# A hybrid short-convolution and RG-LRU layer in fp32r: one output product of the second half made from seven smaller ones, and the order of the opening and of the sweeps

## The chip, the cores and the metric

The kernel runs on one core of one Trainium2 chip. The metric is device microseconds (us) of one execution; the time of a kernel is the median of its runs. The engines are named as the profile names them: PE (TensorE), DVE (VectorE), ACT (ScalarE), POOL (GpSimd), SP (SyncE, which issues transfers here).

## The reference

One layer of a diffusion trunk on 2048 latent tokens of width 1024, with 256 context tokens whose scan states start the latent scans.

```python
shift, scale, gate = split(silu(c) @ w_ada + b_ada, 3)
h  = rmsnorm(x, norm_g) * (1 + scale) + shift            # hc: the same of ctx with c_ctx
v, g_b, g_c, z_a, u, z_b, m_a, m_b = split(h @ w_in)     # eight products 1024 x 1024
xc = grid_conv(u, conv4_w, 2) + conv4_b                  # rows of 64 tokens
r, i = sigmoid(block_diag(xc, wr) + br), sigmoid(block_diag(xc, wi) + bi)   # per direction
a = exp(-8 * r * softplus(-lambda)); y_lru = scan_fwd + scan_bwd of sqrt(1-a*a) * i * xc
y_a = g_b * grid_conv(g_c * v, conv3_w, 1) * silu(z_a)
y_b = y_lru * silu(z_b)
merged = sigmoid(m_a) * (y_a @ w_out_a) + sigmoid(m_b) * (y_b @ w_out_b)
x = rmsnorm(x + gate * (merged @ w_o), final_g)
```

## The kernel before

The tokens lie in four blocks of 512. A tile is 128 channels by 512 tokens. Blocks 0 and 1 are the first half, blocks 2 and 3 the second. Every product is made in fp32r with weights and data split into a high and a low part: high by high, low by high and high by low are added up, so a product with a full inner dimension of 1024 takes 24 matmuls for one output tile (`passes`, line 455).

Where two blocks and both halves of the channels come together, a 2 x 2 scheme with seven products (`Pair`, line 524) takes the place of the eight plain ones. Each of the seven takes 12 matmuls. It needs seven forms of the data: B11, B21 and B22, which are tiles as they are, and T1 to T4, which are differences (T1 = x12-x11, T3 = x22-x12, T2 = x22-T1, T4 = x21-T2). It also needs four weight differences, made by four POOL instructions in `prep_d` (line 540). Loops over such products are `sgemm` (line 1127); loops over plain products are `gemm` (line 1114).

The program goes in this order. (1) The opening: the adaLN rows are made by matvecs with the loaded rows `wc` of w_ada (line 841); block 0 is modulated two channel tiles at a time as its scale and shift arrive (`modulated`); then the plain products aL, aG, aV, aMA, aB, aZA of the first channel tile are made, first with block 0, then with block 1. (2) `sweep(0, c)` for the eight channel tiles c, each with seven products for each of the L, G, B and Z weights, the LRU gates (`bdp`, `Lru.gates`) and the forward scans. (3) The first half's product with w_out_a (`merged_a(0)`), in which the forms of the second half are built. (4) `sweep(1, c)`, with the backward scans of the first half (`back0`) and `gate_step` recorded after each sweep. (5) The second half's product with w_out_a (`merged_a(1)`, names `oa1..`, plain), in which the forms of y_b are built (`build_y`, DVE). (6) `merged_b(1)` with w_out_b (names `ob1..`, seven products), `wo1`, `merged_b(0)`, and the last product with w_o and the output.

Nothing of this runs in the order in which it is recorded. Each call adds an `Op` with an engine and an estimated duration to a `Plan`, and `place` and `once` (lines 125 and 141) list-schedule them: PE keeps the order of recording, the other engines take the ready Op of the lowest priority number, which is the latest time by which the Ops after it need it. Buffers come from slot pools: 17 T slots (fp32 tiles), 64 F slots (fp32r tiles, the data's parts), W, D, R and S for weights, six accumulators. A load is issued no earlier than 18 us ahead of its priority (`AHEAD`).

A form from DRAM is loaded into a T slot; then ACT writes the high part and DVE the low part into two F slots (`put`, line 423).

Of the kernel before, what the change touches and what calls it, by code (L numbers as in the profile page):

```python
# [25 lines left out]

PARAMS = (("g", K), ("bada", 3 * K), ("w3", 3 * K), ("w4", 4 * K), ("b4", K), ("br", 2 * K),
# [45 lines left out]
class Op:  # L73
    def __init__(self, eng, dur, emit, table=None, lat=0.15):
        self.eng, self.dur, self.emit, self.table, self.lat = eng, dur, emit, table, lat
        self.deps, self.succ, self.allocs, self.uses = set(), [], [], []
        self.prio = self.nom = self.start = self.end = 0.0


class Plan:  # L80
# [60 lines left out]
    def once(self):  # L141
# [6 lines left out]
        indeg = {op: len(op.deps) for op in ops}  # L148
# [27 lines left out]
        while len(order) < len(ops):  # L176
            best = None
            now = pe[pe_at].nom if pe_at < len(pe) else 1e9
            for e, c in cand.items():
                pick = None  # L180
                for op in c:
# [3 lines left out]
                    if op.allocs:  # L185
                        if e == "SP" and op.prio > now + AHEAD:
                            continue
# [37 lines left out]
            for b in op.uses:  # L225
                b.left -= 1
                b.end = max(b.end, op.end + op.lat)
                if not b.left and b.pool:
                    insort(slots[b.pool], (b.end, b.slot))
            for s in op.succ:  # L230
# [16 lines left out]
def trunk(ctx: ExitStack, tc: tile.TileContext, par, sel2, xT, ctxT, wada, wgate, crow, win, woa, wob, wo, lru, out):  # L247
# [110 lines left out]
    yb_dram = dram("yb_dram", 2, K, 2, P, T)  # L358
    mg_dram = dram("mg_dram", 2, K, 2, P, T)
# [59 lines left out]
    def split2(hi, lo, x, n=T):  # L419
        A(hi, x, AF.Copy, n=n)  # L420
        TT(lo, x, hi, SU, n)
# [10 lines left out]

    def fetch(name, src, kb=512, after=()):
# [4 lines left out]
    def plain(name, src, after=()):  # L438
        r = fetch("r" + name, src, after=after)
# [4 lines left out]
    def spread(name, src, after=()):  # L444

        r = fetch("r" + name, src, after=after)
# [370 lines left out]
    last = []  # L817

    def wload(m):
        for k in range(K):  # L820
            w = wc[m, k] = tb(f"wc{m}{k}")
            last[:] = [DMA(w.v, wada[m, :, k, :], 256)]

    def xload(name, src):
        r = []
        for k in range(K):
            x = tf(f"{name}{k}")
            last[:] = [DMA(x.v, src[:, k, :], 256, after=[sel_op])]
            r.append(x)
        return r  # L830
# [45 lines left out]
    acc0 = [ps(n) for n in ("aL", "aG", "aV")]  # L876
# [13 lines left out]

    rv = matvec(0)
    wload(1)
    turn(0, rv)
    rv = matvec(1)
    rs0 = s0.rs()
    modulated(0)
    ws0[0] = wL = plain("L00", sL, after=last)
    wload(2)
    turn(1, rv)
    modulated(1)  # L900
    rv = matvec(2)
    ws0[1] = wG = plain("G00", sG, after=last)
    turn(2, rv)
    wload(3)
    ws0[2] = wV = plain("V00", sV, after=last)
    group(0, 0)
    modulated(2)
    group(0, 1)
    rv = matvec(3)
    group(0, 2)  # L910
    turn(3, rv)
    modulated(3)
    wMA = spread("MA00", sMA, after=last)
    wB = spread("B00", sB, after=last)
# [4 lines left out]
    for i in (1, 2):  # L919
        for m in range(H - 1):  # L920
            group(i, m)
    for i in range(3):
# [4 lines left out]
    wZA = spread("ZA00", sZA, after=last)  # L927
    a = unit("aMA0", wMA, bt0)
    merge_gate("sma_dram", 0, 0, 0, a.v)
    rs1 = s1.rs()  # L930
# [14 lines left out]
    for j in range(H):  # L945
        h = tb(f"hcx{j}")
        DMA(h.v, ctxT[:, 2 * j:2 * j + 2, :].rearrange("p k n -> p (k n)"), 256, after=last)
# [3 lines left out]
    a = unit("aB0", wB, bt0)  # L951
    cv.gb(0, a.v)
# [9 lines left out]
    lr.weights(after=last)  # L962
# [31 lines left out]
    def rest(form, kinds, biased=True):  # L994

        for n, i in kinds:
            for j in range(H):
                x = tb(n + "x")
                DMA(x.v, dbuf("fm_dram", i, j), 256)
                form[n].append(put(f"{n}_{j}", x.v, shf(H + j) if i == 2 and biased else None))  # L1000


    def sweep(half, c, state, form):

        plain_start = half == 0 and c == 0
# [10 lines left out]
        else:  # L1016
# [7 lines left out]
            lr.conv(0, l0.v)  # L1024
            pl.p6(form)
            if half == 0:
                lr.ctx_gates(0)
            pl.p5(form)
            if half == 0:
                lr.ctx_gates(1)  # L1030
                lr.ctx_scan()
            ma1 = pl.p7(form)
# [403 lines left out]
```

## Time and profile before

| | before |
|---|---|
| median of 3 runs | 1954.68 us (1952.62 to 1955.51) |
| profiled execution | 1953.45 us |
| its span in the trace | 1951.7 us (1.75 us lie around it) |
| mean granted clock of PE | 0.994 |
| busy: PE, DVE, ACT, POOL | 97%, 81%, 58%, 26% |

The span is what the profiler records from the first to the last instruction. Busy shares are shares of the span. The profile's line numbers are those of the kernel before; in the kernel after, the helpers have moved (the ACT helper from line 264 to 274, tensor-tensor from 270 to 280, matmul from 312 to 322).

### The profile page before, as it was taken

What the parts mean: (1) busy time and instruction counts of PE and PEld (TensorE: products, weight loads), DVE (VectorE), ACT (ScalarE), POOL (GpSimd) and SP (SyncE); (2) the same over time, 40 slices, a digit from 0 to 9 for tenths busy, and PEclk for the clock granted to TensorE, in tenths of its full rate; (3) what the DMA queues carried; (4) which work ended last, traced back from release to release, by engine and by line L of the source; (5) the groups of instructions that cost most, each with busy time, mean ns of one, the idle gap of its engine ahead of it and who ended that gap; (6) DMA issues with size and microseconds to landing.
All of it is one profiled execution on the core that took longest, in us unless ns stands there. A gap on an engine that the chain in (4) does not pass through costs nothing.

```text
span 1951.7 us, 24306 instructions
## 1 busy us (share of the span) xinstructions
PE 1902.7 (97%) x8546; PEld 1562.0 (80%) x8546; DVE 1578.9 (81%) x2044; ACT 1136.3 (58%) x1604; POOL 503.1 (26%) x311
## 2 busy tenths in 40 slices
PE   6989999999999999999999999999999999999997
PEld 3777888888888888888888888888888888788787
DVE  6897878778686878858998989989898778779854
ACT  5587676767677777347565575655747333435332
POOL 1313223322535221023324333233241022012100
PEclk8999999999999999999999999999999999999999
DMA  9252323232433325951433424234243985777933
GB/s 328 75 184 95 124 81 125 79 131 91 161 119 121 124 81 195 325 189 57 157 109 112 146 75 157 92 129 143 69 167 101 334 316 187 271 244 248 328 119 117
DMA packets 145419, 307.89 MB, mean 158 GB/s; under 512 B 16272, under 2 KB 20496, under 8 KB 145296
## 3 DMA queue, kind: packets, MB, share of 16 engines
q1 hardware_dynamic: 145296, 306.34, 45.5%
q8 instruction: 67, 1.10, 0.2%
q14 instruction: 56, 0.46, 0.1%
HBM read 218.19 MB, written 88.08 MB: 157 GB/s over the span
## 4 chain that ended last, share of the span: by engine, by line
PE 68%; DVE 14%; ACT 8%; DMA 6%; issue 3%; SPq 0%; ACTq 0%; DVEq 0%
PE oa L312 9%; PE wo L312 4%; PE ao L312 4%; PE bdp L312 3%; ACT L264 3%; DVE xc L277 2%; DMA pk<-pk_dram 2%; DVE i L296 2%; PE ac L312 1%; DMA wc<-wada 1%; DVE x L277 1%; DMA mg_dram<-sb 1%; DVE y L270 1%; DVE wg L277 1%; DVE i L270 1%
## 5 line engine op out<-in xcount | busy, mean ns | idle before, releaser
L264 ACT ACT_TABLE_LOAD x152 | 195.0, 1283 | 8.1 <-DMA pr<-par 2.7
L296 DVE TENSOR_TENSOR_SCAN i<-a,st,i 128x512 f32<-128x512 f32 x48 | 75.2, 1579 | 0.0
L270 DVE TENSOR_TENSOR i<-i,r 128x512 f32<-128x512 f32 x64 | 66.7, 1042 | 0.1
L277 DVE SCALAR_TENSOR_TENSOR r<-a,r 128x512 f32<-128x512 f32 x64 | 49.2, 789 | 18.1 <-ACT r L264 18.1
L264 ACT ACTIVATE xh<-xc 128x512 fp32r<-128x512 f32 x32 | 20.2, 632 | 61.7 <-DVE xc L277 61.7
L270 DVE TENSOR_TENSOR i<-i,xc 128x512 f32<-128x512 f32 x64 | 50.4, 806 | 0.4 <-ACT i L264 0.4
L264 ACT ACTIVATE a<-r,ns 128x512 f32<-128x512 f32 x64 | 45.9, 720 | 0.8 <-DVE i L270 0.3
L264 ACT ACTIVATE r<-bdp,pr 128x512 f32<-128x512 f32 x64 | 44.0, 687 | 2.1 <-PE bdp L312 0.6
L264 ACT ACTIVATE i<-bdp,pr 128x512 f32<-128x512 f32 x64 | 44.0, 687 | 0.6 <-PE bdp L312 0.6
L264 ACT ACTIVATE r<-r,hs 128x512 f32<-128x512 f32 x64 | 43.1, 712 | 0.0
L277 DVE SCALAR_TENSOR_TENSOR zz<-ao,gates,xr 128x256 f32<-128x256 f32 (+1 forms) x24 | 13.6, 572 | 34.5 <-PE ao L312 32.6
L264 ACT ACTIVATE sq<-zz 128x256 f32<-128x256 f32 (+1 forms) x21 | 10.3, 488 | 49.4 <-DVE zz L277 49.2
L264 ACT ACTIVATE r<-r 128x512 f32<-128x512 f32 x64 | 37.7, 624 | 0.4
L270 DVE TENSOR_TENSOR xl<-xc,xh 128x512 fp32r<-128x512 f32 x32 | 33.4, 1045 | 4.5 <-ACT xh L264 4.5
L270 DVE TENSOR_TENSOR sa<-oa,sa 128x512 f32<-128x512 f32 x32 | 21.7, 686 | 13.3 <-DMA sa<-sma_dram 7.2
L277 DVE SCALAR_TENSOR_TENSOR ri<-acc,ri 128x256 f32<-128x256 f32 x16 | 6.5, 413 | 30.3 <-ACT ri L264 30.3
L270 DVE TENSOR_TENSOR yx<-yx,yx 128x512 f32<-128x512 f32 x32 | 25.3, 790 | 5.0 <-DMA fm_dram<-yx 2.4
L270 DVE TENSOR_TENSOR y<-y,sg 128x512 f32<-128x512 f32 x32 | 29.0, 907 | 0.0
L841 PE MATMUL row<-wc,sc 128*32 128x512 f32 x64 | 15.8, 698 | 9.5 <-DMA wc<-wada 4.9
L270 POOL TENSOR_TENSOR ob00s<-ob00r 128x512 f32<-128x512 f32 x1 | 1.3, 1292 | 91.5 <-DMA fm_dram<-yx 91.5
L296 DVE TENSOR_TENSOR_SCAN pk<-pk,st,pk 128x512 f32<-128x512 f32 x16 | 20.5, 1279 | 5.2 <-DMA pk<-pk_dram 5.2
L270 POOL TENSOR_TENSOR ob10s<-ob10r 128x512 f32<-128x512 f32 x1 | 1.3, 1289 | 89.6 <-DMA ob10r<-wob 89.6
(15371 smaller groups left out, 7391.3 us busy)
## 6 DMA issues: line engine op xcount, KB each, us to landing
pk<-pk_dram SPq DMA_DIRECT2D x48, 256.0 KB, 5.7
wc<-wada SPq DMA_DIRECT2D x32, 256.0 KB, 5.4
ya_dram<-y SPq DMA_DIRECT2D x32, 256.0 KB, 3.4
pk_dram<-i SPq DMA_DIRECT2D x32, 256.0 KB, 2.8
roa<-woa SPq DMA_DIRECT2D x16, 512.0 KB, 4.3
ya<-ya_dram SPq DMA_DIRECT2D x32, 256.0 KB, 5.1
sa<-sma_dram SPq DMA_DIRECT2D x32, 256.0 KB, 5.0
pa_dram<-sa SPq DMA_DIRECT2D x32, 256.0 KB, 5.0
```

The source lines that it names most:

```text
L264: act.activation(o.ap(), i.ap(), func, **kw)
L270: return plan.add(Op(eng, d, lambda: e.tensor_tensor(o.ap(), a.ap(), b.ap(), op=op)), [o], [a, b])
L277: dve.scalar_tensor_tensor(o.ap(), a.ap(), s.ap() if isinstance(s, V) else s, b.ap(), op0=op0, op1=op1, **kw)
L296: dve.tensor_tensor_scan(o.ap(), a.ap(), u.ap(), init.ap() if isinstance(init, V) else init, op0=M, op1=AD)
L312: pe.matmul(o.ap(), w.ap(), x.ap(), start=a, stop=z, skip_group_check=True)
L841: pe.matmul(row.fixed[32 * j:32 * j + 32, :], w.ap(), x.ap(), start=a, stop=z, skip_group_check=True, tile_position=(0, 32 * j))
```

## The change

It has five parts.

1. The second half's product with w_out_a becomes an `sgemm` of seven products (`merged_a1`). The forms of y_a come from `combine("ya", j)`: four loads, four POOL subtractions and four stores to `yat_dram`, recorded inside the sweeps 5, 6 and 7 for j = 0 to 2; for j = 3 they are made on DVE from tiles still in SBUF. The forms of y_b for `merged_b(1)` come in the same way from `combine("yb", j)`, inside the sweeps 6 and 7 and inside the product, and no longer from `build_y` on DVE. Forms are loaded when they are first asked for, two kinds ahead (`LEAD`), and the low part of j = 1 is made on POOL (`POOLED`).
2. `put_from` loads a form into the F slot of its own low part and not into a T slot.
3. `sweep` takes a list of steps, and `back0`, `gate_step` and `combine` are recorded between its products.
4. In the opening all loads are chained in one order (`queue`): block 0, the first w_ada rows, then weights and rows in turn, and block 1 behind the last rows. The products aMA and aB take part, in groups of two channel tiles, as the modulation arrives. The sums of squares of block 1 move from POOL to DVE.
5. In `sweep(0, 0)` the last gates and forward scan (`late`) are recorded behind the next sweep's first tail product.

```diff
+            if op.heir:
+                op.prio = min(p, op.heir.prio)
...
+    def put_from(name, src, bias=None, eng="DVE"):
+
+        lo, hi = fb(name + "l"), fb(name + "h")
+        raw = lo.m(lambda t: t.bitcast(F32))
+        DMA(raw, src, 256)
+        if bias is None:
+            split2(hi.v, lo.v, raw, eng=eng)
...
+    def queue(op):
+
+        if line:
+            line[-1].heir, op.heir_of = op, line[-1]
+        op.dur *= 0.84
+        line.append(op)
+        return op
...
-    acc0 = [ps(n) for n in ("aL", "aG", "aV")]
+    rL, rG = raw0("L00", sL), raw0("G00", sG)
+    acc0 = [ps(n) for n in ("aL", "aG", "aV", "aMA0", "aB0")]
...
+    rMA = raw0("MA00", sMA)
+    wload(3)
     rv = matvec(2)
...
+    rB = raw0("B00", sB)
     rv = matvec(3)
+    group(3, 0)
     turn(3, rv)
+    group(3, 1)
+    for i in range(4):
+        group(i, 2)
+    ws0[4] = wB = spread("B00", sB, rB)
     modulated(3)
+    for m in range(H - 1):
+        group(4, m)
     x1 = xload("x1_", xT[1])
-    s1 = Stats("x1", eng="POOL")
+    s1 = Stats("x1")
...
+            def late(first=state["tail"][0]):
+                first()
+                lr.gates(1, 1)
+                lr.decay(1)
+                lr.forward(1)
+            state["tail"][0] = late
...
+        for i, (o, a, b) in enumerate(((x11, x12, x11), (x12, x22, x12), (x22, x22, x11), (x21, x21, x22))):
+            TT(o, a, b, SU, eng="DVE" if late else "POOL")
+            if not late:
+                DMA(dbuf(f"{key}t_dram", (0, 2, 1, 3)[i], j), o, 256)
...
     for c in range(K):
-        sweep(1, c, state, form1)
-        if c + 1 < K:
-            gate_step(c)
-            back0(2 * c)
-            back0(2 * c + 1)
+        side = []
+        if c:
+            side = [lambda: back0(2 * c - 2), lambda: gate_step(c - 1), lambda: back0(2 * c - 1)]
+        if c > H:
+            side.insert(1, lambda: combine("ya", c - H - 1))
+        if c > H + 1:
+            side.insert(3, lambda: combine("yb", c - H - 2))
+        sweep(1, c, state, form1, side)
+    y7 = combine("ya", H - 1, [state["cv"].y[t] for t in range(2)])
...
-        if n in (2, 5, 8, 11):
-            build_y(1, n // 3, forms_y[1])
-
-    merged_a(1, ya, between_a)
-    rest(forms_y[1], (("T3", 1), ("T4", 0), ("B22", 2)), False)
-    mg = merged_b(1, forms_y[1], lambda n: None)
+    merged_a1(Forms("ya", y7), between_a)
+    mg = merged_b(1, Forms("yb"), lambda n: None)
```

The order on the engines moves most at three places. The first is ACT in the opening, where `B_0h` and `B_1h` are the high parts of the third pair of block 0's channel tiles, `sq` the squares, and `rows_431` and `rows_494` the copy of the fourth adaLN row. Before, it stands so:

```order
L264 ACTIVATE B_0h<-x_4_188,ab 128x512
L264 ACTIVATE B_1h<-x_5_192,ab 128x512
L264 ACTIVATE V00h<-rV_351 128x1024
L264 ACTIVATE rows_431<-row_389 128x512
L264 ACTIVATE sq<-x_3_366 128x512
L264 ACTIVATE MA000h<-rMA_364 128x512
```

After, it stands so (`ZA000h` is a weight's high part):

```order
L274 ACTIVATE sq<-x_4_347 128x512
L274 ACTIVATE sq<-x_5_351 128x512
L274 ACTIVATE sq<-x_6_354 128x512
L274 ACTIVATE B_0h<-x_4_127,ab 128x512
L274 ACTIVATE B_1h<-x_5_129,ab 128x512
L274 ACTIVATE sq<-x_7_363 128x512
L274 ACTIVATE rows_494<-row_458 128x512
L274 ACTIVATE ZA000h<-rZA_369 128x512
```

The copy of the fourth row stood ahead of block 1's squares 3 to 7; now it stands behind all eight of them.

The second place is POOL in the last sweep and at the start of the second half's w_out_a product. Before, the four differences of the last Z weights are followed by those of the first w_out_b weights:

```order
L270 TENSOR_TENSOR Z17r_12085<-Z17s_12185,Z17r_12085 128x512
L270 TENSOR_TENSOR Z17r_12085<-Z17r_12085 128x512
L270 TENSOR_TENSOR ob10s_13091<-ob10r_13038 128x512
L270 TENSOR_TENSOR ob10r_13038<-ob10r_13044,ob10r_13038 128x512
```

After (`cx` are the tiles of `combine`, `yaB` and `yaT` the parts of y_a's forms, `oa10r` the raw w_out_a weights):

```order
L280 TENSOR_TENSOR Z17r_12121<-Z17s_12233,Z17r_12121 128x512
L280 TENSOR_TENSOR Z17r_12121<-Z17r_12121 128x512
L280 TENSOR_TENSOR yaB_1l<-yaB_1l,yaB_1h 128x512 x2
L280 TENSOR_TENSOR oa10s_12461<-oa10r_12412 128x512
L280 TENSOR_TENSOR oa10r_12412<-oa10r_12320,oa10r_12412 128x512
L280 TENSOR_TENSOR yaT_1l<-yaT_1l,yaT_1h 128x512
L280 TENSOR_TENSOR oa10r_12320<-oa10s_12461,oa10r_12320 128x512
L280 TENSOR_TENSOR yaT_1l<-yaT_1l,yaT_1h 128x512
L280 TENSOR_TENSOR oa10r_12320<-oa10r_12320 128x512
L280 TENSOR_TENSOR yaT_1l<-yaT_1l,yaT_1h 128x512 x2
L280 TENSOR_TENSOR cx_12571<-cx_12575,cx_12571 128x512
```

Between the last Z weights and the first w_out_b weights POOL now makes low parts of the forms, the differences of four pairs of w_out_a weights and subtractions of y_b.

The third place is DVE at the start of that product. Before (`ya_0k` are the plain tiles of y_a, `Z17a`, `Z17u` and `y` the last steps of the last sweep):

```order
L270 TENSOR_TENSOR ya_05l<-ya_05_12434,ya_05h 128x512
L270 TENSOR_TENSOR ya_06l<-ya_06_12453,ya_06h 128x512
L270 TENSOR_TENSOR Z17a<-Z17a,zs_12423 128x512
L270 TENSOR_TENSOR y_12217<-y_12217,sg_12340 128x512
L270 TENSOR_TENSOR Z17a<-Z17a,i_170_12087 128x512
L270 TENSOR_TENSOR Z17u_12374<-Z17z,Z17u_12374 128x512
```

After:

```order
L280 TENSOR_TENSOR y_12263<-y_12263,sg_12472 128x512
L280 TENSOR_TENSOR cx_12470<-cx_12503,cx_12470 128x512
L280 TENSOR_TENSOR yaB_0l<-yaB_0l,yaB_0h 128x512
L280 TENSOR_TENSOR yaB_2l<-yaB_2l,yaB_2h 128x512
L280 TENSOR_TENSOR yaB_3l<-yaB_3l,yaB_3h 128x512
L280 TENSOR_TENSOR cx_12503<-y_12263,cx_12503 128x512
L280 TENSOR_TENSOR oa10Bl<-oa10r_12320,oa10Bh 128x1024
L280 TENSOR_TENSOR y_12263<-y_12263,cx_12470 128x512
L280 TENSOR_TENSOR yaT_0l<-yaT_0l,yaT_0h 128x512
L280 TENSOR_TENSOR yaT_2l<-yaT_2l,yaT_2h 128x512
```

The chain of differences of j = 3 (`cx`, then `y`) now lies on DVE between the last sweep and the product, with the low parts of the forms among it.

## Rows read from the trace of the kernel before

**Rows 1.** The page's busy time, share of the span and instructions of each engine.

```profile
PE 1902.7 (97%) x8546; PEld 1562.0 (80%) x8546; DVE 1578.9 (81%) x2044; ACT 1136.3 (58%) x1604; POOL 503.1 (26%) x311
```

**Rows 2.** Stretches: opening, end of sweeps, second w_out_a product; last: clock, DMA share, GB/s.

```profile
0.00:200.00 200.00, 173.74 (x740) 128.90 (x741) 152.86 (x254) 137.26 (x210) 47.37 (x37) 0.96 0.49 168
900.00:1508.00 608.00, 606.05 (x2667) 499.95 (x2667) 554.35 (x664) 369.99 (x500) 200.59 (x116) 1.00 0.35 118
1508.00:1599.00 91.00, 91.00 (x404) 75.32 (x403) 67.44 (x97) 31.31 (x46) 7.50 (x6) 1.00 0.90 326
```

**Rows 3.** The chain that ended last, PE: start, time, of what.

```profile
1510.98 87.04 PE oa L312 x384
1646.98 2.73 PE ob12y L312 x12
```

**Rows 4.** Stretches of the first 40 us, columns as in rows 2.

```profile
0.00:20.00 20.00, 9.84 (x35) 2.83 (x36) 9.83 (x46) 8.73 (x14) 0.20 (x4) 0.97 0.92 314
20.00:40.00 20.00, 16.54 (x62) 7.78 (x65) 11.98 (x23) 11.30 (x15) 2.07 (x2) 0.69 1.04 392
```

**Rows 5.** Timeline of ACT and PE, opening: start, mean of one, instruction, [wait <-releaser].

```profile
44.31 0.58 ACT L264 ACTIVATE rows<-row 128x512 f32<-128x512 f32 x1
46.34 2.18 ACT L264 ACTIVATE sq<-x 128x512 f32<-128x512 f32 x4
...
76.55 0.58 PE L312 MATMUL aL<-B_0h,L00h 128*128 128x512 f32 x1
79.05 0.50 PE L312 MATMUL aL<-B_1l,L00h 128*128 128x512 f32 x1 [1.01 <-DVE B_1l L277]
84.06 0.50 PE L312 MATMUL aL<-B_3l,L00h 128*128 128x512 f32 x1 [0.63 <-DVE B_3l L277]
141.57 0.78 PE L312 MATMUL bdp<-xh,bw00h 128*128 128x512 f32 x1 [4.97 <-ACT r L264]
```

**Rows 6.** Stretches of PE alone: length, busy, granted clock, DMA share, GB/s.

```profile
34.00:36.00 2.00, 1.28 (x4) 0.50 1.06 398
140.00:142.00 2.00, 0.43 (x1) 0.91 0.00 0
142.00:144.00 2.00, 2.00 (x6) 0.50 0.28 102
144.00:146.00 2.00, 2.00 (x9) 0.74 0.95 294
```

**Rows 7.** Timeline of DVE and POOL near the end of the last sweep, columns as in rows 5.

```profile
1470.45 0.48 DVE L283 TENSOR_SCALAR y<-G17a,pr 128x512 f32<-128x512 f32 x1
1475.49 1.28 POOL L270 TENSOR_TENSOR Z17s<-Z17r 128x512 f32<-128x512 f32 x1 [13.35 <-DMA Z17r<-win]
1475.78 2.08 DVE L270 TENSOR_TENSOR Z17Al<-Z17r,Z17Ah 128x1024 fp32r<-128x1024 f32 x1
1477.78 1.77 DVE L270 TENSOR_TENSOR G17u<-G17u,G17u 128x512 f32<-128x512 f32 x1
1479.48 1.77 DVE L270 TENSOR_TENSOR i<-i,r 128x512 f32<-128x512 f32 x1
1481.18 1.52 DVE L283 TENSOR_SCALAR y<-G17u,pr 128x512 f32<-128x512 f32 x1
1492.06 0.69 DVE L270 TENSOR_TENSOR i<-i,r 128x512 f32<-128x512 f32 x1
1495.18 1.23 DVE L270 TENSOR_TENSOR Z17Cl<-Z17r,Z17Ch 128x1024 fp32r<-128x1024 f32 x1
```

**Rows 8.** Stretches of the sweeps 5, 6 and 7 and of the product, columns as in rows 2.

```profile
1256.00:1338.00 82.00, 81.57 (x360) 67.25 (x359) 74.50 (x89) 49.47 (x67) 27.70 (x17) 1.00 0.34 119
1338.00:1420.00 82.00, 82.00 (x364) 67.91 (x363) 74.62 (x91) 49.70 (x68) 27.13 (x17) 1.00 0.34 119
1420.00:1508.00 88.00, 87.00 (x383) 71.44 (x382) 78.97 (x101) 52.58 (x73) 22.97 (x14) 1.00 0.38 126
1508.00:1588.00 80.00, 80.00 (x355) 66.23 (x354) 60.45 (x83) 27.38 (x40) 5.88 (x4) 1.00 0.89 322
```

More of the change, by code (lines that the diff above doesn't have):

```diff
@@ L185, in once @@
                     if op.allocs:
-                        if e == "SP" and op.prio > now + AHEAD:
+                        if e == "SP" and op.prio > now + AHEAD and not op.heir_of:
                             continue
@@ L821, in wload @@
             w = wc[m, k] = tb(f"wc{m}{k}")
-            last[:] = [DMA(w.v, wada[m, :, k, :], 256)]
+            queue(DMA(w.v, wada[m, :, k, :], 256))
     def xload(name, src):
@@ L827, in xload, with raw0 @@
             x = tf(f"{name}{k}")
-            last[:] = [DMA(x.v, src[:, k, :], 256, after=[sel_op])]
+            queue(DMA(x.v, src[:, k, :], 256))
             r.append(x)
+        return r
+    def raw0(name, src):
+        r = Buf("R", "r" + name)
+        queue(DMA(r.v, src, 512))
         return r
@@ L946, in trunk @@
         h = tb(f"hcx{j}")
-        DMA(h.v, ctxT[:, 2 * j:2 * j + 2, :].rearrange("p k n -> p (k n)"), 256, after=last)
+        queue(DMA(h.v, ctxT[:, 2 * j:2 * j + 2, :].rearrange("p k n -> p (k n)"), 256))
         hcs.append(h)
@@ L961, in trunk @@
             DMA(dbuf("hc_dram", k // 2), hcs[k // 2].v, 256)
-    lr.weights(after=last)
+    lr.weights()
     acc1 = [ps(n) for n in ("aL1", "aG1", "aV1")]
@@ L997, in rest, with sweep, step @@
             for j in range(H):
[L998 to L1003, printed above, removed]
+                form[n].append(put_from(f"{n}_{j}", dbuf("fm_dram", i, j), shf(H + j) if i == 2 and biased else None))
+    def sweep(half, c, state, form, side=()):
+        side = list(side)
+        def step():
+            if side:
+                side.pop(0)()
         plain_start = half == 0 and c == 0
@@ L1024, in sweep @@
             lr.conv(0, l0.v)
+            step()
             pl.p6(form)
@@ L1149, in sgemm, with combine, __init__, more @@
         use(H - 1, 1, c12.v, c12.v, n + 1)
+    def combine(key, j, late=None):
+        xs = []
+        for k, t in ((j, 0), (j, 1)) + (() if late else ((H + j, 0), (H + j, 1))):
+            x = tb(f"cx{k}{t}")
+            DMA(x.v, dbuf(f"{key}_dram", 1, k, t), 256)
+            xs.append(x.v)
+        x11, x12, x21, x22 = xs + (late or [])
+        for i, (o, a, b) in enumerate(((x11, x12, x11), (x12, x22, x12), (x22, x22, x11), (x21, x21, x22))):
+            TT(o, a, b, SU, eng="DVE" if late else "POOL")
+            if not late:
+                DMA(dbuf(f"{key}t_dram", (0, 2, 1, 3)[i], j), o, 256)
+        return {"T1": x11, "T3": x12, "T2": x22, "T4": x21}
+    class Forms(dict):
+        def __init__(self, key, last=()):
+            self.last = last
+            b, t = f"{key}_dram", f"{key}t_dram"
+            self.key = key
+            self.todo = [("B11", lambda j: dbuf(b, 1, j, 0)), ("B21", lambda j: dbuf(b, 1, H + j, 0)),
+                         ("T2", lambda j: dbuf(t, 1, j)), ("T1", lambda j: dbuf(t, 0, j)),
+                         ("T3", lambda j: dbuf(t, 2, j)), ("T4", lambda j: dbuf(t, 3, j)),
+                         ("B22", lambda j: dbuf(b, 1, H + j, 1))]
+        def more(self):
+            name, src = self.todo.pop(0)
+            self[name] = [put(f"{self.key}{name}_{j}", self.last[name]) if j == H - 1 and name in self.last else
+                          put_from(f"{self.key}{name}_{j}", src(j), eng="POOL" if POOLED(name, j) else "DVE") for j in range(H)]
+        def __getitem__(self, name):
+            while name not in self:
+                self.more()
+            ahead = 0
+            while self.todo and ahead < LEAD:
+                self.more()
+                ahead += 1
+            return dict.__getitem__(self, name)
+    def merged_a1(form, between):
+        def use(d, t, a, own, n):
+            s = tb("sa")
+            DMA(s.v, dbuf("sma_dram", 1, d, t), 256)
+            TT(s.v, a, s.v, M)
+            DMA(dbuf("pa_dram", 1, d, t), s.v, 256)
+            between(n)
+        sgemm("oa1", woa, form, use)
     def merged_a(half, ya, between):
```

94 lines of the change are left out of this document (52 added, 42 removed).

## The prediction

> **What bounds the kernel now.** I read the busy times first: PE is busy 97% of the span and DVE 81%, while ACT and POOL are far below [rows 1]. Shares over a whole span mix stages, so next come the stretches. In the opening PE is busy 173.74 of 200 us, and that is where most of its idle time lies; in the sweeps of the second half it is busy 606.05 of 608, and in the second half's w_out_a product 91.00 of 91 [rows 2]. The chain of waits says the same for that product: 384 matmuls of `oa` stand on it as one piece of 87.04 us, and the seven-product loop behind it follows in pieces of 12 matmuls, 2.73 us each [rows 3]. So PE is the bound behind the first 200 us, and a matmul taken away there is worth its whole time, provided that what feeds PE keeps up. DVE is the engine to watch: 554.35 of 608 us in the sweeps [rows 2]. In the opening the bound is the adaLN chain (loads, rows, modulation), and the timeline shows PE waiting for DVE and ACT there [rows 5].
>
> All sums are made against the profiled execution of 1953.45 us (span 1951.7 and 1.75 around it), which lies 1.23 below the median of the three runs. I take 0.2% (3.9 us) as what a measurement of this kernel can tell from no change.
>
> **Fewer matmuls.** Each of eight output rows and two blocks took 24, which is 384. Four pairs of seven products of 12 are 336, so 48 go. At 87.04/384 = 0.2267 us [rows 3] that is **-10.9 us**. DMA traffic rises by about 14 MB, most of it form loads and stores in the last sweeps and in the product. The sweeps move 118 GB/s, the product 326 [rows 2], and the first 40 us show 392 [rows 4]; the first w_out_b pairs behind the product need less. I take 0 for it, with the room to 392 as its cover; without it a late form would stall PE by a load at a time.
>
> **The opening, rows and modulation.** Before, blocks and rows stood in one order, with weights behind the rows. Now one chain of loads runs x0, wc0, L, G, wc1, V, wc2, MA, wc3, B, x1, ZA: 12.7 MB up to the last row of w_ada, 15.3 up to the last tile of x1. The first 20 us move 314 GB/s, 6.28 MB; the next 20 run at 392 [rows 4]. So the last row is there at 20 + 6.4/0.392 = 36.4 us and x1 at 43.0. ACT then decides: its copy of the fourth row began at 44.31 [rows 5], and the order now puts it behind all eight of block 1's squares, each about 0.55 us (2.18 for four). With x1 at 43.0 the copy starts near 45.3, a microsecond later than before. What is gained is what PE does in the meantime: of block 0's 144 matmuls, 42 (seven groups of six) stand before the fourth row's modulation and not 18. 24 x 0.2267 = 5.4 us less behind it. Against this stands the clock. After idle time PE's granted clock shows 0.50 in 34 to 36 us and in 142 to 144, and 0.74 in 144 to 146 [rows 6]: the low one of the two levels (1.2 and 2.4 GHz) lasts some microseconds. Waiting for the modulation with its work done, PE could lose up to 3.2 us that way. I take **-3.5**, between 0 and -7. The six additions of squares that go from POOL to DVE (6 x 0.68 = 4.1 us) are covered by DVE's idle 47 of 200 us [rows 2]; without that cover block 1's modulation is 4.1 us later.
>
> **The opening, late gates.** PE waits 4.97 us for ACT before the last gate matmuls at 141.57, and runs at 0.50 behind it [rows 5, 6]. With `late`, the context products (about 3.45 us), a 2.7 us block of L01 and the 12 matmuls of the Z tail come first: 8.9 us of work that needs none of these gates. The wait goes, and with it about 1.6 us of the low clock: **-6.5**. The bounds are -1, if the forward scan moved back becomes late for whoever reads it (the backward scan and `zb`), and -7. What is late next is the scan on DVE; it is not read until the next sweep's end.
>
> **POOL against DVE.** The change gives POOL 28 subtractions of y_a and y_b, 9 low parts of forms and 16 weight differences between the fifth sweep and the w_out_b product: 53 instructions. DVE's own work there hardly changes: `build_y` goes, the forms' low parts and j = 3's differences come, together about +2 us. But the two engines disturb each other. While POOL made four differences at the end of the last sweep, DVE's four instructions beside them took 2.08, 1.77, 1.77 and 1.52 us, where the same shapes take 1.23, 0.69, 0.69 and 0.48 when POOL is still [rows 7]. That is 7.14 against 3.09: 4.05 us of DVE time for four POOL instructions, 1.01 each. One that meets an idle DVE costs nothing. DVE is busy 228.1 of 252 us in the three sweeps, and 60.45 of 80 in the product [rows 8]; weighted so, the 20 in the sweeps cost 0.91 each and the 33 in the product 0.77. But these stretches fill up, which brings them nearer to 1.01; I take p = 0.85. The lower bound is half of a lone POOL instruction, 0.64 of 1.28 us [rows 7], if each side gives way in turn. DVE's room is what is idle in the four stretches, 332 - 288.5 = 43.5 us [rows 8], less the 10.9 that the product gets shorter: 32.6. So PE waits 53 x 0.85 + 2 - 32.6 = **+14 us**, +3 at 0.64 and +23 at 1.01. What stands behind DVE is the forms' low parts, which PE needs at blocks of 2.7 us each from the product's first matmul on. That all room can be used is an assumption; idle time that lies where nothing is ready is lost.
>
> The Trainium skill (page "SBUF — State Buffer", section "Who interferes with whom") says that an elementwise instruction of VectorE with two SBUF inputs contends with a GpSimd instruction that reads SBUF, and that the second to come is held until the first is done, not slowed. The rows agree on the first; on the second, DVE lost about 1.0 and not the whole 1.28 of a lone POOL instruction. By the page's rule the sum here would be 53 x 1.28 + 2 - 32.6 = +37.
>
> **Form loads in the low parts' slots, scans recorded inside the sweeps.** A form no longer holds one of the 17 T slots. PE's idle time in the sweeps is 2 of 608 us [rows 2], so there is next to nothing to win and, while PE's order is kept, a late scan delays only its readers. I take **0**; the bounds are -2, all that is idle, and +2, a stall of half a microsecond at each of four product starts like the smallest wait of [rows 5].
>
> **The sum.** -10.9 - 3.5 - 6.5 + 14 + 0 = -6.9: 1946.5 for an execution like the profiled one, and about 1947 to 1948 by the median. I say **1947**.
>
> **The rivals.**
>
> B, contention hides: the additional POOL work meets DVE at 0.64 or less. Speaking for it: DVE has 43.5 us of idle time there [rows 8]. Against: [rows 7]. Then -20.9 + 3 or less, 1934 to 1937; with the opening at its best about 1930.
>
> C, the other side: DVE becomes the bound from the fifth sweep to the w_out_b product, since each POOL instruction costs it 1.05 us or more. From p = 1.05 on the sum is +3.9: -20.9 + 2 + 55.7 - 32.6 = +4.2, 1959; at 1.1 it is +6.8, 1961.5. [Rows 7] with 1.01 are close to it, and the gates need the scans in time; against it, most of the new instructions are in the product, where DVE is least busy. The page's rule above would be this case at its far end, +16 and 1971; with 1.01 measured against 1.28 I give that end 0.03 of C's chance.
>
> D, the opening does not do what it says: the copy of the fourth row waits for block 1's squares, the low clock takes what the 24 matmuls give, and the gates' wait moves to the next product. For it: ACT's order. Against: 4.97 us of wait are seen [rows 5]. Then -10.9 + 14 = +3, 1957.
>
> **How the numbers follow.** The forecast (A) covers p from 0.7 to 0.95 with the opening at -5 to -13: 1938 to 1953; chance 0.45. B 0.25, C 0.18, D 0.12. Faster by over 0.2%, below 1950.8: all of B and 0.36 of A, 0.61. Within 0.2%: 0.09 of A and 0.10 of D, 0.19. Slower: C and 0.02 of D, 0.20. The range 1930 to 1962 holds B but for its best end and C up to p = 1.1. Faster alone would be 1930 to 1950.
>
> **What would show it.** The `oa1` product as 28 blocks of 12 matmuls in the chain of waits, about 76 us if nothing is late; with contention, waits of PE for DVE on `yaT`, `yaB` and `oa1` low parts, and DVE instructions of that shape near 1.7 us beside POOL. DVE's busy share in the stretches of [rows 8] near 98% with PE's share falling says C; PE's share unchanged says B. In the opening, `aL` of block 1 near 73 and not 76.55, and no wait at the gates near 135 to 141. I would be wrong if the forms' loads or stores arrive late (PE waiting on a DMA), or if PE idles in the sweeps for a scan that was recorded later than before.

## The result and the profile after

The changed kernel takes 1988.1 us (1986.78 to 1989.47, 4 runs) against 1955.1 before (also 4 runs, one more than in the table of before): a ratio of 1.0167 with a 95% interval of 1.0153 to 1.0181. It is 33 us slower. The forecast was 1947, in a range of 1930 to 1962. The profiled execution has a span of 1985.0 us, 33.3 more than before.

The first matmul of each stage in the two timelines says where these 33.3 us arise:

| stretch | before | after | difference | forecast |
|---|---|---|---|---|
| start to first matmul of the second half's sweeps (L10) | 854.25 | 847.08 | -7.2 | -10 |
| sweeps 0 to 4 of the second half (to L15) | 404.03 | 406.41 | +2.4 | 0 |
| sweeps 5 to 7 (to oa10) | 252.54 | 282.37 | +29.8 | part of the next |
| product with w_out_a (to ob10) | 87.04 | 95.38 | +8.3 | -10.9 + 14 for both |
| the rest | 353.84 | 353.76 | -0.1 | 0 |

For comparison, the three sweeps of the kernel before on these bounds (stretches, columns as in [rows 2]):

```profile
1258.28:1510.82 252.54, 251.12 (x1106) 207.04 (x1104) 228.62 (x282) 153.77 (x210) 75.59 (x45) 1.00 0.36 125
```

Then the changed kernel, first the page's busy time of each engine, which answers to [rows 1]:

```profile
PE 1905.5 (96%) x8498; PEld 1560.0 (79%) x8498; DVE 1632.3 (82%) x2056; ACT 1156.2 (58%) x1638; POOL 608.3 (31%) x363
```

and its stretches that answer to [rows 2, 8]: the opening, the three sweeps, the product:

```profile
0.00:200.00 200.00, 177.04 (x774) 134.56 (x775) 161.15 (x270) 144.75 (x217) 41.72 (x32) 0.97 0.49 170
1253.49:1535.86 282.37, 262.37 (x1105) 212.46 (x1104) 253.49 (x279) 159.84 (x223) 132.32 (x76) 0.96 0.48 164
1535.86:1631.24 95.38, 82.94 (x337) 65.89 (x336) 83.29 (x92) 37.82 (x57) 57.31 (x31) 0.95 0.78 277
```

The 48 matmuls are gone, and yet PE is busy longer than in [rows 1]. In the three sweeps it makes the same matmuls in 262.37 instead of 251.12 us, at a mean clock of 0.96, and stands idle for 20.0 us instead of 1.4. So 18.6 of the 29.8 us are waits, and 11.3 are matmuls at the lower clock. In the product 336 matmuls at 0.2267 would be 76.2 us; they take 82.94, and PE is idle for 12.4 more. DVE is not full, at 253.49 of 282.37 us. The five longest waits for which PE stands in these stretches (engine, what waited, for whom: sum, times, longest):

```profile
PE G17y L322 <- ACT G17u L274: 6.0, 1, 6.0
PE G16y L322 <- ACT G16u L274: 5.0, 1, 5.0
PE oa13z L322 <- DVE oa13u L280: 4.1, 1, 4.1
PE oa10y L322 <- ACT oa10u L274: 3.6, 1, 3.6
PE oa10z L322 <- DVE oa10u L280: 2.5, 1, 2.5
```

`G16u` is ACT's copy that empties an accumulator; before, no wait of PE in this stretch is over 0.7 us. PE itself waits for a DMA only once in the whole run, for 0.6 us in the opening. In sweep 6 a subtraction of `combine` on POOL (`cx`) and a DVE instruction beside it look like this; the DVE instruction takes 0.68 us when POOL is still:

```profile
1362.95 1.73 POOL L280 TENSOR_TENSOR cx<-cx,cx 128x512 f32<-128x512 f32 x1
1363.46 1.77 DVE L280 TENSOR_TENSOR pk<-pk,szl 128x512 f32<-128x512 f32 x1
```

What then holds `G16u` is shown by the timeline of DVE, ACT and PE:

```profile
1379.84 0.70 DVE L287 SCALAR_TENSOR_TENSOR xc<-L16u,pr,xc 128x496 f32<-128x496 f32 x1
...
1383.86 1.77 DVE L287 SCALAR_TENSOR_TENSOR xc<-L16u,pr,xc 128x504 f32<-128x504 f32 x1
...
1387.24 0.73 DVE L287 SCALAR_TENSOR_TENSOR xc<-L16u,pr,xc 128x504 f32<-128x504 f32 x1
1388.07 0.63 ACT L274 ACTIVATE xh<-xc 128x512 fp32r<-128x512 f32 x1 [6.12 <-DVE xc L287]
...
1391.73 0.58 ACT L274 ACTIVATE G16u<-G16y 128x512 f32<-128x512 f32 x1
1392.36 0.79 PE L322 MATMUL G16y<-T_0h,G16Ch 128*128 128x512 f32 x1 [5.03 <-ACT G16u L274]
```

The convolution `xc` is late on DVE. ACT, which takes its instructions in order, waits 6.12 us for it, and the copy that PE needs stands behind. PE then pays a second time, by its granted clock (stretches of PE alone, columns as in [rows 6]):

```profile
1390.00:1392.00 2.00, 0.00 (x0) 0.76 0.00 0
1392.00:1394.00 2.00, 1.64 (x4) 0.50 0.03 8
1394.00:1396.00 2.00, 2.00 (x7) 0.50 0.00 0
1396.00:1398.00 2.00, 2.00 (x7) 0.53 0.00 0
1398.00:1400.00 2.00, 2.00 (x10) 1.00 0.00 0
```

After the wait, from 1392.36 to 1398, the granted clock is 0.50 to 0.53. The twelve matmuls of the first product there take 5.3 us, to 1397.65; at 0.2267 each they would take 2.7. So a wait of 5 us costs some 2.6 more.

In the product the timeline shows something that the kernel before has nowhere (POOL, DVE, ACT and PE):

```profile
1545.70 10.24 POOL L280 TENSOR_TENSOR yaB_1l<-yaB_1l,yaB_1h 128x512 fp32r<-128x512 f32 x1 [8.11 <-ACT yaB_1h L274]
...
1557.14 1.25 POOL L280 TENSOR_TENSOR oa11s<-oa11r 128x512 f32<-128x512 f32 x1
...
1545.82 0.68 DVE L280 TENSOR_TENSOR Z17a<-Z17a,i 128x512 f32<-128x512 f32 x1
...
1554.11 0.68 DVE L280 TENSOR_TENSOR yaT_2l<-yaT_2l,yaT_2h 128x512 fp32r<-128x512 f32 x1
...
1558.43 0.63 ACT L274 ACTIVATE oa11Dh<-oa11s 128x512 fp32r<-128x512 f32 x1 [9.68 <-POOL oa11s L280]
...
1559.48 0.58 ACT L274 ACTIVATE oa10u<-oa10y 128x512 f32<-128x512 f32 x1
1560.11 0.50 PE L322 MATMUL oa10y<-yaT_0h,oa10Ch 128*128 128x512 f32 x1 [3.58 <-ACT oa10u L274]
```

One POOL subtraction stands 10.24 us. Between the two DVE rows DVE makes two-input instructions one behind the other, at their full speed of 0.68 and 1.21 us, until 1554.8; POOL ends 1.1 us later. The w_out_a sum behind it is late, ACT waits 9.68 us for that sum, and PE 3.58 us for the copy behind ACT's wait. The longest wait in the product, 4.1 us at `oa13z`, is another: there DVE's instructions beside POOL's take 1.75 to 1.78 us again, and `oa13u` comes late behind four of them.

The opening did gain. The waits that answer to [rows 5] (PE and ACT):

```profile
132.88 0.50 PE L322 MATMUL bdp<-xh,bw00h 128*128 128x512 f32 x1 [3.13 <-ACT ri L274]
...
146.00 0.39 PE L322 MATMUL bdp<-xh,bw00h 128*128 128x512 f32 x1
...
48.25 0.58 ACT L274 ACTIVATE rows<-row 128x512 f32<-128x512 f32 x1
```

The late gates at 146.00 wait for nothing, in place of 4.97 us; but the gates ahead of them now wait 3.13, where they waited 0.35 before. The copy of the fourth row is at 48.25, 3 us later than forecast and 3.9 later than before.

### The profile page after: what moved, and what is told of

It reads as the page before. It is cut to its first block, busy times and chain, and to the rows that moved or that the text cites. A ratio compares the mean times of both kernels' runs of the same rounds, so it can differ in the third digit from the quotient of the medians.

```text
span 1985.0 us, 24392 instructions
## 1 busy us (share of the span) xinstructions
PE 1905.5 (96%) x8498; PEld 1560.0 (79%) x8498; DVE 1632.3 (82%) x2056; ACT 1156.2 (58%) x1638; POOL 608.3 (31%) x363
## 5 line engine op out<-in xcount | busy, mean ns | idle before, releaser
L306 DVE TENSOR_TENSOR_SCAN i<-a,st,i 128x512 f32<-128x512 f32 x48 | 80.4, 1687 | 0.0
L280 POOL TENSOR_TENSOR cx<-cx,cx 128x512 f32<-128x512 f32 x28 | 50.9, 1819 | 36.4 <-DMA cx<-ya_dram 24.8
L274 ACT ACTIVATE r<-r,hs 128x512 f32<-128x512 f32 x64 | 43.5, 711 | 0.0
L274 ACT ACTIVATE sq<-zz 128x256 f32<-128x256 f32 (+1 forms) x21 | 10.2, 489 | 50.1 <-DVE zz L287 47.5
L287 DVE SCALAR_TENSOR_TENSOR xcc<-ac,pr,xcc 128x255 f32<-128x255 f32 (+1 forms) x24 | 11.5, 480 | 14.0 <-ACT xcc L274 13.5
L280 POOL TENSOR_TENSOR hcss<-hcss,sq 128x256 f32<-128x256 f32 x7 | 7.4, 1056 | 50.6 <-ACT sq L274 50.2
```

The costliest lines, as they stand in the source:

```text
L274: act.activation(o.ap(), i.ap(), func, **kw)
L280: return plan.add(Op(eng, d, lambda: e.tensor_tensor(o.ap(), a.ap(), b.ap(), op=op)), [o], [a, b])
L287: dve.scalar_tensor_tensor(o.ap(), a.ap(), s.ap() if isinstance(s, V) else s, b.ap(), op0=op0, op1=op1, **kw)
L306: dve.tensor_tensor_scan(o.ap(), a.ap(), u.ap(), init.ap() if isinstance(init, V) else init, op0=M, op1=AD)
```

## The experiments

The theories: **P**, the new POOL instructions make DVE late, and lateness becomes PE waits. **S**, the scans and gate steps recorded inside the sweeps stand at worse places. **F**, the forms' loads and slots. Later came **Q**, a held POOL instruction stalls the product, and **R**, idle DVE time is room only where it lies (against **P0**, that each subtraction costs the same anywhere). The runs from e5 on follow from what the earlier ones left open.

**e1, the opening alone** (with late; the rest of the change put back):

```diff
-        sweep(1, c, state, form1, side)
+        sweep(1, c, state, form1)
+        if c + 1 < K:
+            gate_step(c)
+            back0(2 * c)
+            back0(2 * c + 1)
...
-    merged_a1(Forms("ya", y7), between_a)
+    merged_a(1, ya, between_a)
```

> Only the opening's part of the change (chained loads, products in groups, squares on DVE, late gates) on the kernel before; the rest as before. In the changed kernel the first matmul of the sweeps' second tile and everything up to the second half stands 7.2 to 7.7 us earlier than before. All theories expect that gain to last to the end: 1946 to 1949 us against 1955. A time near 1955 would say that the gain of the opening is given back behind it whatever else is changed.

Measured: 1949.57 us against 1955.13, ratio 0.9969 (0.9957 to 0.998). The gain of the opening lasts; at 5.6 us it is a little smaller than the stage table has it, and the time lies just above the range that I had given.

**e2, no subtractions inside the sweeps.**

```diff
-            TT(o, a, b, SU, eng="DVE" if late else "POOL")
+            if late or not quiet:
+                TT(o, a, b, SU, eng="DVE" if late else "POOL")
...
-            side.insert(1, lambda: combine("ya", c - H - 1))
+            side.insert(1, lambda: combine("ya", c - H - 1, None, True))
```

> The changed kernel with the 20 POOL subtractions inside the sweeps 5 to 7 left out (the tiles are loaded and stored unsubtracted, so the forms T1 to T4 of these are not the reference's). Theory P (each of these POOL instructions takes the shared SBUF access from DVE, and DVE's lateness stalls PE): the 32 us that the sweeps 2 to 7 lose go nearly all, 1954 to 1962 us. Theory S (the scans and gate steps recorded inside the sweeps come at worse places): still above 1980 us. Theory F (loads and slots of the forms): above 1980 us too, since all loads and stores stay.

Measured: 1968.54, ratio 1.0075 (1.0058 to 1.0093), 19.6 us less than the changed kernel. By the first matmuls of its trace, the sweeps 5 to 7 lose 10.5 us against the kernel before and not 29.8: 19.3/20 = 0.97 us for each subtraction. P holds for two thirds of that loss. The time is above the range that I had given for P, since 10.5 us stay. The product is as long as in the changed kernel, 95.5 us.

**e3, the subtractions on DVE; e4, the steps ahead of the sweep.**

```diff
-            TT(o, a, b, SU, eng="DVE" if late else "POOL")
+            TT(o, a, b, SU, eng="DVE")
```
```diff
-        sweep(1, c, state, form1, side)
+        for f in side:
+            f()
+        sweep(1, c, state, form1)
```

> The changed kernel with all 28 subtractions of combine on DVE and none on POOL. Theory P: DVE gets 28 x 0.68 = 19 us more of its own, and is freed of 28 collisions, which cost PE some 1.6 us each in the sweeps: 1962 to 1975 us. If a collision costs only what the subtraction itself would cost on DVE, no change, 1985 to 1990. Theory S: DVE is later still, 1990 to 2000 us.

> The changed kernel with the backward scans, the gate steps and the subtractions recorded between the sweeps (as the scans were before) and not inside them. Theory S: most of the 32 us come back, 1956 to 1968 us. Theory P: the same POOL instructions meet the same DVE, 1983 to 1993 us.

Measured: e3 1973.48, ratio 1.0089 (1.0066 to 1.0113), as P had it; e4 1986.17, ratio 1.0158 (1.0134 to 1.0182). S is not the cause of the loss. In e3's trace the three sweeps take 268.2 us in place of 282.4, and the product 88.5 in place of 95.4, although a POOL instruction is held there for 10.24 us as well; 3.5 us of the gain are lost again behind the product.

**e5, the plain product with the steps inside the sweeps; e7 and e8, POOL work put into e5.** e5 takes `merged_a(1)` and `build_y` back and drops `combine`. e7 adds to it, at the places of `combine`:

```diff
+    def dummy(j, t):
+        x = tb("dx")
+        DMA(x.v, dbuf("ya_dram", 1, j, t), 256)
+        for _ in range(4):
+            TT(x.v, x.v, x.v, SU, eng="POOL")
```

In e8 the last line is `plan.add(Op("POOL", 1.58, lambda: pool.memset(x.v.ap(), 0.0)), [x.v], [])`.

> The changed kernel with the plain product and the DVE-built forms of y_b put back, but with the scans and gate steps recorded inside the sweeps, the forms loaded into the low parts' slots, and the new opening. Theory P (POOL's new instructions are the loss): as fast as the run with the opening alone, 1947 to 1951 us. Theory S (scans at worse places) or F (slots): 1953 us or more, with waits in the sweeps 2 to 4, where the changed kernel already lost 3 us before any subtraction.

> The kernel of e5 with five groups of four POOL subtractions put into the sweeps 5 to 7, at the places of combine: each group has one load of 256 KB and subtracts the tile from itself, with no use of the result. Theory P: 20 x 0.97 us (the price from leaving them out of the changed kernel), 17 to 22 us above e5, 1965 to 1972. If DVE's idle time takes them up, as the prediction had it, 0 to 4 above e5. If the loads, stores and slots of combine were what cost, 0 to 4 too.

> As e7, with POOL memsets of the same tile in place of the subtractions: POOL writes SBUF and reads nothing. By the Trainium skill's rule (page SBUF — State Buffer, section Who interferes with whom) an instruction that only writes does not meet DVE's second input: as e5, within 2 us. If any POOL access costs DVE time: above e5 in proportion to POOL's busy time.

Measured: e5 1951.31, ratio 0.9972 (0.9959 to 0.9985), at the upper end of what P gave: without the new product and its POOL work the loss is gone. e7 1967.63, ratio 1.0062 (1.0046 to 1.0079), 16.3 above e5, 0.82 us for each subtraction: 16.3 of the 19.3 us that e2 gave back arise with POOL subtractions and five loads, without `combine`'s other loads, its stores and its tiles. e8 1957.75, ratio 1.001 (0.9998 to 1.0022), 6.4 above e5, where I had expected 2 at most. Its timeline shows both kinds side by side, first DVE, then POOL:

```profile
1272.06 1.78 DVE L280 TENSOR_TENSOR pk<-pk,pk 128x512 f32<-128x512 f32 x1
1273.77 1.78 DVE L287 SCALAR_TENSOR_TENSOR xc<-L15a,pr,xc 128x504 f32<-128x504 f32 x1
...
1277.18 0.68 DVE L280 TENSOR_TENSOR pk<-pk,szl 128x512 f32<-128x512 f32 x1
...
1272.01 1.28 POOL L280 TENSOR_TENSOR G15r<-G15r,G15r 128x512 f32<-128x512 f32 x1
1273.24 0.53 POOL L1389 MEMSET dx<- 128x512 f32 x1
1273.72 1.28 POOL L280 TENSOR_TENSOR G15r<-G15s,G15r 128x512 f32<-128x512 f32 x1
```

DVE's instruction that begins 0.05 us after POOL's subtraction takes 1.78 us: it ends about 0.55 us after POOL's 1.28 are over, beside the memset. Here POOL is first, and DVE is held until it is done. This is the exclusive lock of the Trainium skill (page "SBUF — State Buffer", section "Who interferes with whom"), and the memset beside it is not stretched, as that section says of an instruction that only writes. The held subtraction at 1545.70 looks like the same lock the other way round: a DVE instruction was under way when it began. Why the two take turns in one place and DVE keeps the access for 9 us in another no run here settles; nor did a run take e8's 6.4 us apart.

**e6, e9, e10, e11, the product.** e6 leaves out the 16 w_out_a sums and differences; e9 sets `POOLED = lambda n, j: False`; e10 puts all the new work on DVE; e11 leaves the product without new POOL work.

```diff
+            if n.startswith("oa"):
+                DMA(s.v, self.s1[:, :H, :], 256)
+                self.fd = Buf("D", n + "Dh"), Buf("D", n + "Dl")
+                split2(self.fd[0].v, self.fd[1].v, s.v)
+                return
```

> The changed kernel without the 16 POOL sums and differences of the w_out_a weights (one plain half is loaded in place of the D weights and the others are taken as they are, so the product is not the reference's). Theory P: the product, which took 95.4 us from its first matmul to the first of w_out_b instead of 76, gets 10 to 16 us shorter: 1971 to 1978 us. If the product is late for its forms and accumulators alone, it stays within 4 us of the changed kernel, 1983 to 1990.

> The changed kernel with the low parts of the forms' second tiles (j = 1) on DVE and not on POOL. In its trace, and in three runs more, one of these POOL instructions stood 10.2 us while DVE made 14 two-input instructions one behind the other, and PE, ACT and the w_out_a weights waited behind it. Theory Q (that held instruction is the product's stall): 6 to 10 us shorter, 1978 to 1983, with no POOL instruction above 4 us there. If the next POOL instruction (a w_out_a sum) is held in its place: 1985 to 1990. If DVE's own work is what stalls the product: 1988 to 1994, since it gets 6 us more.

> The changed kernel with none of the new work on POOL: subtractions of combine, low parts of j = 1 and sums and differences of the w_out_a weights all on DVE, some 53 x 0.68 = 36 us of DVE time. Theory P (a POOL instruction costs more than the same on DVE) with Q: below the run that moves the 28 subtractions alone (1973 us), 1962 to 1972. If DVE is full: above it, 1976 to 1990. Against the kernel before it is slower by all theories, since the 36 us exceed the room of 32.6.

> The changed kernel with no new POOL work in the product: low parts of j = 1 on DVE, the four subtractions of y_b for j = 2 and 3 left out, the w_out_a weights without sums and differences (so neither product is the reference's); the sweeps keep their subtractions. Theories P and Q: the product takes 76 to 82 us and not 95.4: 1968 to 1975 us. If the forms' low parts, ACT's copies or late loads are what stalls it, it stays above 88 us: 1981 or more.

Measured: e6 1987.93, ratio 1.0169 (1.0152 to 1.0186), no gain: P's 10 to 16 us were wrong. e9 1985.09, ratio 1.0147 (1.012 to 1.0174). In both the product takes 97.0 us, and another POOL instruction stands in place of the held one, first the row of e6, then of e9:

```profile
1528.37 18.86 POOL L280 TENSOR_TENSOR yaT_1l<-yaT_1l,yaT_1h 128x512 fp32r<-128x512 f32 x1 [1.57 <-ACT yaT_1h L274]
```
```profile
1536.81 19.91 POOL L280 TENSOR_TENSOR cx<-cx,cx 128x512 f32<-128x512 f32 x1 [6.85 <-DMA cx<-yb_dram]
```

So taking away either the weights' sums or the low parts does not help. Taking away all of it does: e10 is 1966.19, ratio 1.0047 (1.0029 to 1.0064), and e11 1975.14, ratio 1.0094 (1.0077 to 1.0111). In e11 no POOL instruction takes over 2.2 us in that stretch, and the product takes 82.2 us in place of 95.4. P and Q together account for 13 of the 19.2 us that the product takes over 76.2; 4.7 of the 13 come back behind the product. Even so it is only 4.8 us shorter than the plain product, with work left out. Q alone is not shown: e3, which among the product's POOL work has only `combine`'s subtractions moved, keeps a held instruction and takes 88.5 us, about as long as e10 without any new POOL work (89.0).

**e12, the same 20 subtractions as e7 on DVE** (against e7):

```diff
-            TT(x.v, x.v, x.v, SU, eng="POOL")
+            TT(x.v, x.v, x.v, SU)
```

> As e7 (20 subtractions of a loaded tile from itself in the sweeps 5 to 7 of the kernel of e5), on DVE and not on POOL: 20 x 0.68 = 13.6 us of DVE time. Theory P: much less than e7's 16 us above e5, 0 to 6 us (1951 to 1957), since DVE's idle time takes them up and no collision arises. If DVE's time is simply full there: 10 to 14 above, 1961 to 1965.

Measured: 1965.21, ratio 1.0041 (1.0028 to 1.0053), 13.9 above e5, 0.70 us each, which is all of DVE's own 0.68. I was wrong here: without any collision the work still costs its full time, so at these places the idle time took nothing up. On POOL the same 20 cost 16.3.

**e13 and e14, 12 subtractions at two places.** The stretches of e5's sixth sweep show where DVE is idle (columns as in [rows 2]):

```profile
1365.20:1373.40 8.20, 8.20 (x38) 6.80 (x37) 7.71 (x13) 4.87 (x7) 0.55 (x1) 1.00 0.56 188
1373.40:1381.60 8.20, 8.20 (x38) 6.80 (x37) 8.13 (x8) 4.86 (x8) 6.12 (x4) 1.00 0.09 36
1381.60:1389.80 8.20, 8.20 (x38) 6.80 (x37) 3.40 (x6) 7.62 (x11) 0.00 (x0) 1.00 0.01 2
1389.80:1398.00 8.20, 8.20 (x38) 6.76 (x37) 8.20 (x9) 4.40 (x5) 3.88 (x3) 1.00 0.38 128
```

DVE is full in three of these four slices and idle for 4.8 us in one, in which POOL has nothing to do and ACT makes the gates. e13 puts four subtractions of each sweep there, e14 among the G weights' differences. The edit of e13 (the list names the last POOL instruction recorded so far, behind which the four have to stand):

```diff
             b0 = pb.p2(form)
+            if half and c > H:
+                dummy(c - H - 1, [[o for o in plan.ops if o.eng == "POOL"][-1]])
```

> The kernel of e5 with 12 POOL subtractions (each group of four subtracts a loaded tile from itself, with no use of the result), four in each of the sweeps 5 to 7, placed behind the B weights' differences. In the trace of the kernel before, DVE is busy 8.1 to 8.2 of 8.2 us in most slices of a sweep and 3.6 of 8.2 in the one slice that follows these differences. Theory R (DVE's idle time is only room where it lies): nearly free, 0 to 4 us above e5, 1950 to 1955. Theory P0 (each POOL subtraction costs PE some 0.9 us wherever it is): 9 to 13 above, 1960 to 1965.

> As e13, the same 12 POOL subtractions, recorded at the first place of combine, where they stand among the G weights' differences and DVE is busy all the time. Theories R and P0: 9 to 13 us above e5, 1960 to 1965. If it is the number of them in one sweep that counts (four against eight in e7), 0 to 4 above.

Measured: e13 1951.64, ratio 0.9976 (0.9965 to 0.9986), 0.3 above e5. e14 1959.48, ratio 1.0019 (1.0009 to 1.0028), 8.2 above e5, 0.68 each, a little less than I had given. The same instructions cost next to nothing at one place and 8 us at the other: R holds. The waits of PE in e13, which are those of e5:

```profile
PE L16y L322 <- ACT L16u L274: 1.3, 1, 1.3
PE L17y L322 <- ACT L17u L274: 1.3, 1, 1.3
PE Z17y L322 <- ACT Z17u L274: 0.7, 1, 0.7
```

and in e14 the three that are new:

```profile
PE G17y L322 <- DVE G17Bl L280: 2.5, 1, 2.5
PE G16y L322 <- DVE G16Bl L280: 2.2, 1, 2.2
PE G15y L322 <- DVE G15Bl L280: 1.9, 1, 1.9
```

In e13 DVE and POOL do collide; its timeline of DVE shows it:

```profile
1380.27 1.52 DVE L280 TENSOR_TENSOR B16Dl<-B16s,B16Dh 128x512 fp32r<-128x512 f32 x1
1381.71 1.52 DVE L280 TENSOR_TENSOR i<-i,xc 128x512 f32<-128x512 f32 x1
...
1386.13 0.69 DVE L280 TENSOR_TENSOR G16a<-G16y,G16a 128x512 f32<-128x512 f32 x1 [2.29 <-PE G16y L322]
```

but 2.29 us of idle time are left behind it, so nothing that follows is late.

**e17, y_a's own subtractions at the idle place** (in the changed kernel, with the hook of e13 and `combine("ya", ...)`):

> The changed kernel with the 12 POOL subtractions of y_a in the sweeps 5 to 7 placed behind the B weights' differences, ahead of DVE's idle stretch, as in e13; those of y_b stay at the busy place. Theory R: 12 x 0.7 to 0.9 us come back, 1976 to 1981 us against 1988. Theory P0: no change, 1985 to 1990. If the four tiles that each group holds, and not the collisions, stall the sweep: no change either.

Measured: 1973.52, ratio 1.0086 (1.0069 to 1.0102), 14.6 below the changed kernel, more than expected, with twelve instructions moved and none taken away. Its trace has the three sweeps at 264.3 us in place of 282.4 and the product at 98.4 in place of 95.4. That is more for each instruction than any price above, and no run says why.

**e15, everything but the seven products and the steps; e16, the same without late.**

```diff
+        if not pg:
+            lr.gates(1, 1)
+            lr.decay(1)
+            lr.forward(1)
...
-            def late(first=state["tail"][0]):
```

> The new opening and the form loads in the low parts' slots, with the plain product, build_y and the scans recorded between the sweeps: all of the change but its seven products and its steps inside the sweeps. In the run with the steps (e5) PE waits 1.3 us for ACT at the start of each sweep, in the run with the opening alone it does not. If the steps cause these waits: 1945 to 1949 us. If the slots cause them: 1950 to 1953.

> As e15, with the last gates and forward scan of the first sweep recorded where they were before (late undone). The trace of the changed kernel puts 2.3 us of the opening's gain ahead of these gates and 4.9 behind: 4 to 6 us above e15. If the gates' wait were only moved to a later place by late, 0 to 2 above.

Measured: e15 1945.99, ratio 0.9954 (0.9942 to 0.9967), the fastest of all kernels here. e16 1956.06, ratio 1.0 (0.9991 to 1.0009): 10 us above e15, more than expected, and no gain over the kernel before. In e16 block 1's first matmul of aL starts at 74.33, 2.2 us earlier than in [rows 5]; but the first gates then wait 3.15 us for ACT, and the last gates start at 142.56, 1.0 later than before.

## Why the prediction was wrong

**Fewer matmuls: right.** 336 matmuls, 10.9 us less of work; the time went elsewhere.

**The room: the step that failed.** I took DVE's idle time over four stretches, 43.5 us less 10.9, as room of 32.6 that would take up POOL's price before PE waits. Where the work was put there was next to none. e12 costs all of its DVE time, e14 costs 0.68 us for each subtraction, and e13, with the same work where DVE is idle, nothing. [Rows 8] are sums over a sweep of 82 us. Slices of 8.2 us of the same trace show where the idle time lies, here three of sweep 6 (columns as in [rows 2]):

```profile
1370.80:1379.00 8.20, 8.20 (x38) 6.80 (x37) 8.13 (x8) 5.47 (x9) 5.58 (x4) 1.00 0.38 125
1379.00:1387.20 8.20, 8.20 (x38) 6.80 (x37) 3.66 (x5) 7.85 (x12) 1.05 (x1) 1.00 0.01 2
1387.20:1395.40 8.20, 8.20 (x38) 6.80 (x37) 8.13 (x10) 3.46 (x5) 2.04 (x2) 1.00 0.38 128
```

Of the 7.4 us that DVE is idle in this sweep, 4.5 lie in the one slice. The prediction did say that the use of all room was an assumption; it gave it no price. The room is not nothing for work on DVE itself: e10, with all 53 instructions there, is 14.9 us above e5 with 10.9 us less of matmuls, so 25.8 us are paid for some 36 us of work. The changed kernel pays 36.8 + 10.9 = 47.7 us by the same sum.

**The price of a POOL instruction: about right.** I took 0.85 us; e2 gives 0.97 and e7 0.82 for each subtraction in the sweeps. In the product it failed as a price: which POOL work is taken away there matters more than how much (e3 against e6 and e9), and an instruction is held for 10 to 20 us, which the kernel before does not have and which I did not consider. The lock that the Trainium skill states (page "SBUF — State Buffer", section "Who interferes with whom"), which I weighed as the far end of a rival, is what e8's rows show. I had read a loss of 1.0 and not 1.28 us as speaking against it; e8's held instruction loses 1.1, so the two agree. The time, 1988, lies beyond the 1971 that the rival gave at that end; that sum, too, took off the 32.6 of room.

**The sum.** Without the room my own gross term, 53 x 0.85 + 2 = 47 us, comes near what the sweeps 5 to 7 and the product lost, 29.8 + 19.2 = 49 us. That is partly chance: 11.3 and 6.7 us of the 49 are matmuls at the lower clock behind waits, a term that I had in the opening but not here, and e2 leaves 10.5 us in the sweeps without the subtractions. Of these, 5.5 lie between the first matmul of the last Z product and the product's first. e5, without `combine`, has 1.9 of the 10.5; the other 8.6 appear only with `combine`'s loads and stores and the product's forms and weights, and no run took them apart.

**The opening: the size nearly right, the parts wrong.** -10 was forecast, 5.6 measured (e1) to 9.8 (e15). The chained loads and grouped products were to give 3.5 and give nothing by themselves (e16 against the kernel before): the first gates start at 131.92 against 132.20 before, so the wait there takes up what is gained. `late` was to give 6.5 and gives 10 (e16 against e15). In the changed kernel aL of block 1 starts at 75.52, not near 73.

**Steps and slots: 0 forecast.** e5 has a wait of 1.3 us for ACT in each sweep from 1 to 4, 6 and 7, which e15 has only in part (none over 1.0), and is 5.3 us slower by the medians. The six traces that have the sweeps 0 to 4 of e5 (e5, e7, e8, e12, e13, e14) show 405.8 to 409.0 us there, e15 and e16 405.0 and 405.4. So the steps cost something; whether it is more than the bound of 2 is not settled, since the intervals of e5 and e15 overlap. The slots cannot be told from zero (e1 against e15: the intervals overlap too).

**Rivals.** C, DVE as the bound, had the right sign and the right place, but it got there by a price of 1.05 us or more, where the room was what failed. DVE is not full in the changed kernel, so it is not the bound as C meant it: it is late at the places where ACT and PE stand behind it. D came half true: the copy of the fourth row is late and the wait moved, to the gates ahead of the late ones, but the opening still gains. B, that contention hides, holds only at e13's place.

## What to carry to other kernels

Idle time of an engine is room only where it lies: before work is put on an engine that is 90% busy, cut the stretch into slices as short as the work between two waits, and put it into the idle one. Moving elementwise work from DVE to POOL did not take it off DVE where both read SBUF with two inputs: 20 subtractions cost 16.3 us on POOL and 13.9 on DVE, and all 53 instructions 47.7 against 25.8. The two hold each other up, and a POOL instruction behind a run of DVE's was held for the whole run. In an in-order queue the price of lateness is paid by what stands behind it, and PE pays again at the lower clock.

## What the runs showed that I had not expected

A POOL subtraction of 1.28 us was held for 10.1 to 10.2 us (in the changed kernel, e2, e3, e4 and e17), 18.9 (e6) and 19.9 us (e9), while DVE ran at full speed. In the sweeps it is DVE that is held instead, 0.68 becoming 1.78 us (e8). Some kernels' runs spread over more than the others': e5 from 1945.0 to 1955.9 in ten runs, so that differences of 2 us against it mean little.
